# Second mixer of a decoder trunk: which engine splits the weights, which rows are split ahead, and the order of the recurrence's tasks

## The chip, the cores and the metric

One core of a Trainium2 chip runs the whole program. The metric is device time in microseconds (us), the median of several runs; span is the profiled execution from its first to its last instruction.

## The reference

Two layers over 512 positions of width 1024. Each has a mixer and a mixture of experts (MoE). The change is in the mixer of layer 1:

```python
def mixer_rglru(h, w_in, conv_w, conv_b, w_a, b_a, w_x, b_x, lam, w_out):
    gate, xr = jnp.split(h @ w_in, [D_RNN], axis=-1)
    gate = jax.nn.gelu(gate)
    xr = causal_conv(xr, conv_w) + conv_b          # width 4, per channel
    xh = xr.reshape(bsz, t_len, LRU_HEADS, LRU_HEAD_DIM)   # 8 heads of 128
    r = jax.nn.sigmoid(jnp.einsum('bthi,hij->bthj', xh, w_a).reshape(bsz, t_len, D_RNN) + b_a)
    i = jax.nn.sigmoid(jnp.einsum('bthi,hij->bthj', xh, w_x).reshape(bsz, t_len, D_RNN) + b_x)
    log_a = (LRU_C * r.astype(jnp.float32)) * jax.nn.log_sigmoid(lam.astype(jnp.float32))
    a = jnp.exp(log_a)
    b = jnp.sqrt(-jnp.expm1(2.0 * log_a)) * (i * xr).astype(jnp.float32)
    _, hseq = lax.associative_scan(combine, (a, b), axis=1)   # h = a * h + b along positions
    return (gate * hseq.astype(h.dtype)) @ w_out
...
    x = x + mixer_rglru(rms_norm(x, norm_mix_g[1]), ...)      # layer 1
    x = x + hierarchical_moe(rms_norm(x, norm_ffn_g[1]), ...) # 32 experts, 2 of 8 in one of 4 groups
return rms_norm(x, norm_final_g)
```

## The kernel before

Activations lie with channels on the 128 partitions and positions along the row. Dense products keep float32's accuracy by splitting both operands into a high part (rounded to fp32r) and a low part (the rest), and adding three products: high x high, high x low, low x high. The high part of a block of weight rows (`wh`, 128 x 512) is a cast on ScalarE (line 401), the low part (`wl`) a subtraction (line 402) on VectorE or GpSimd, as the argument `lo` says.

The input projection of the second mixer (`mixer1`) has four units of 512 output columns, in the order 2, 3, 0, 1; units 2 and 3 are the recurrence's branch (heads 0 to 3 and 4 to 7), 0 and 1 the gate's. A unit (`unit`) is eight steps, one for each block of 128 weight rows; a step is 12 matmuls (line 445), three products for each of four PSUM banks. Units use banks 0 to 3 and 4 to 7 in turn. Weights come from HBM in halves of a unit (four blocks of rows) through a ring of ten buffers, in the fixed order of a list; an entry for another buffer (`D1`, ...) waits until the program says that it is free.

Tasks of the recurrence are put between the steps: `later` puts a task in a queue with a cost, and after each step `pump` runs tasks until a budget is spent; `flush` runs what is left at the unit's end. `queue` gives the slots by hand, one slot a step. Each engine works its instructions in the order in which they are written, so this sets the order on all engines. For head h the tasks are `c` (bias and taps of the convolution: ScalarE's line 590, three passes of VectorE's line 593 that read the unit's bank), `g` (two gate products in float32, line 601, which reuse banks of the unit before, and two tanh on ScalarE, line 605), `d` (two exponentials on ScalarE, lines 611 and 612, three VectorE passes, 614 to 616), `w` (three VectorE passes, 620 to 622), `roots` (four square roots on ScalarE, line 626, between loads of its function tables) and `s` (a product and the scan on VectorE, 630 and 631). `gated` (`e`) multiplies a scan by its gelu (637 on ScalarE, 638 on VectorE) and splits the result for the output projection (474 on ScalarE, 475).

The output projection (`project`) is made of pieces of 12 matmuls (line 701), by 128 output columns and half of the heads: heads 0 to 3 for columns 0 and 1, then heads 4 to 7 for the same, and so on. The router and the experts of layer 1 follow; their weights (1 MB for each entry) are next in the list, the first for `D1`, which in the mixer holds `xc` of heads 4 to 7. The mixer's buffers have tags: `w0` to `w3` for splits in turn, `q0` to `q3` and `Q` for tanh, `C0`, `C1` and `D0` for the results' high and low parts.

Of the kernel before, what the change touches and what calls it, by code (L numbers as in the profile page):

```python
# [9 lines left out]
F32R = mybir.dt.float32r  # L10
# [3 lines left out]
AF = mybir.ActivationFunctionType  # L14
# [4 lines left out]
P = 128  # L19
T = 512  # L20
NT = 4
D = 1024
NJ = 8
# [16 lines left out]
def hybrid_trunk(ctx: ExitStack, tc: tile.TileContext, x, norm_mix_g, norm_ffn_g, norm_final_g,  # L40
# [5 lines left out]
    V, A, G, TE, SY = nc.vector, nc.scalar, nc.gpsimd, nc.tensor, nc.sync  # L46
# [79 lines left out]
    def take(kind, u):  # L126
        while stream[pos[1]][3] == "C1":
            pos[1] += 1
        k, v, _, _ = stream[pos[1]]
        assert (k, v) == (kind, u), (k, v, kind, u)  # L130
        pos[1] += 1
        t, slot = ring.popleft()
        used.append(slot)
        return t
# [73 lines left out]
    def warm(func):  # L208

        A.activation(dummy, one, func)  # L210
# [125 lines left out]
    class Normed:  # L336
# [23 lines left out]
        def begin(self):  # L360
            wake(3, WAKE[4])
            self.make(0)
            self.make(1)
            for j in range(2, NJ + 1):
                later(lambda j=j: self.make(j), 2)
# [27 lines left out]

    par = [0]

    def split(w, lo):
        par[0] += 1
        shape = [P, *w.shape[1:]]
        wh = big.tile(shape, F32R, tag=f"w{par[0] % 2}", name="wh")
        wl = big.tile(shape, F32R, tag=f"w{par[0] % 2 + 2}", name="wl")  # L400
        A.copy(wh, w)  # L401
        lo.tensor_tensor(wl, w, f(wh), op=OP.subtract)  # L402
        return wh, wl

    first = {}

    def ahead(kind, u, lo=V):

        w = take(kind, u)
        first[kind, u] = w, split(w[:, 0, :], lo)  # L410

    def unit(kind, u, b0, step, budget=1.9, begin=lambda: None, lo=V, then=lambda: None):

        o = [bank(b0 + m, f"pu{m}") for m in range(4)]
        if (kind, u) not in first:
            ahead(kind, u, lo)
        w, nxt = first.pop((kind, u))
        begin()
        for j in range(NJ):
            wh, wl = nxt  # L420
            if j + 1 < NJ:
                if j % 4 == 3:
                    w = take(kind, u)
                nxt = split(w[:, (j + 1) % 4, :], lo)
            else:
                then()
            if j % 4 == 3:
                done()
            step(o, wh, wl, j, j == 0, j == NJ - 1)
            pump(budget)  # L430
        flush()
        return o

    def first_out(kind):
        w = take(kind, 0)
        first[kind, 0] = w, split(w[:, :, 0:P], V)

    def columns_of(n, low=1):

        def step(o, wh, wl, j, first, last):  # L440
            products = [(wh, n.hh), (wl, n.hh)]
            products.insert(low, (wh, n.hl))
            for i, (a, b) in enumerate(products):
                for m in range(4):
                    TE.matmul(o[m], a[:, m * P:(m + 1) * P], b[:, j, :], start=first and i == 0, stop=last and i == 2)  # L445
        return step
# [9 lines left out]
    class Y:  # L456
# [13 lines left out]
        def lo(self, j):  # L470
            return self.part("D0", 4, j) if j < 4 else self.part("JK"[j // 2 - 2], 2, j % 2)
# [98 lines left out]
    def mixer1(rstd):  # L570
        n = Normed(rstd, cols[:, 88:96], 4)
        y = Y()
        step = columns_of(n)
        tags = ("t20", "t21", "sm1", "sm2")
        wax = []

        def recurrence(h0, o):

            hs = range(h0, h0 + 4)
            if h0:  # L580
                d1 = big.tile([P, 4, T], F32, tag="D1", name="xc")
                xc = {h: d1[:, h - h0, :] for h in hs}
            else:
                jk = [big.tile([P, 2, T], F32, tag=t, name="xc") for t in "JK"]
                xc = {h: jk[h // 2][:, h % 2, :] for h in hs}
            tr, ti, tt, ths = {}, {}, {}, []

            def conv(h):
                m = h - h0
                A.activation(xc[h], o[m], AF.Identity, scale=cols[:, 40 + h:41 + h], bias=cols[:, 48 + h:49 + h])  # L590
                for k in (2, 1, 0):
                    d = 3 - k
                    V.scalar_tensor_tensor(xc[h][:, d:], o[m][:, :T - d], cols[:, 16 + 8 * k + h:17 + 8 * k + h],
                                           xc[h][:, d:], op0=OP.mult, op1=OP.add)

            def gates(h):
                if not wax:
                    wax.append(aside.popleft())
                for g, th in enumerate((tr, ti)):
                    pg = bank(h0 + (h - h0) // 2 * 2 + g, "pgate")  # L600
                    TE.matmul(pg, wax[0][:, g, h, :], xc[h], start=True, stop=True)
                    if (h - h0, g) == (2, 0):
                        ths.extend(four(T, "th"))
                    th[h] = ths[2 * (h - h0) + g - 4] if h - h0 > 1 else buf(2 * (h - h0) + g, (T,), "th")
                    A.activation(th[h], pg, AF.Tanh, scale=0.5, bias=half[:, 8 * g + h:8 * g + h + 1])

            def decay(h):


                tt[h] = big.tile([P, T], F32, tag=tags[h - h0], name="tt")  # L610
                A.activation(tt[h], tr[h], AF.Tanh, scale=lc[:, 0, h:h + 1], bias=lc[:, 0, h:h + 1])
                A.activation(tr[h], tr[h], AF.Exp, scale=lc[:, 1, h:h + 1], bias=lc[:, 1, h:h + 1])
                q = tr[h]
                V.tensor_scalar(q, q, 0.5, 0.5, op0=OP.mult, op1=OP.add)
                V.scalar_tensor_tensor(ti[h], ti[h], 1.0, xc[h], op0=OP.add, op1=OP.mult)
                V.scalar_tensor_tensor(xc[h], tt[h], 1.0, q, op0=OP.add, op1=OP.mult)

            def newton(h):
                q = tr[h]
                V.scalar_tensor_tensor(q, xc[h], 2.0, q, op0=OP.subtract, op1=OP.mult)  # L620
                V.tensor_tensor(ti[h], ti[h], q, op=OP.mult)
                V.tensor_scalar(q, q, -2.0, -1.0, op0=OP.mult, op1=OP.add)

            def roots():
                for h in hs:
                    A.activation(tt[h], tt[h], AF.Sqrt)
                warm(AF.Gelu_apprx_tanh if h0 else AF.Exp)

            def scan(h):
                V.scalar_tensor_tensor(ti[h], ti[h], -1.0, tt[h], op0=OP.mult, op1=OP.mult)  # L630
                V.tensor_tensor_scan(xc[h], tr[h], ti[h], 0.0, op0=OP.mult, op1=OP.add)

            return conv, gates, decay, newton, roots, scan, xc

        def gated(h, o, hs, lo=V):
            if h in hs:
                A.activation(o[h % 4], o[h % 4], AF.Gelu_apprx_tanh)
                V.tensor_tensor(hs[h], o[h % 4], hs[h], op=OP.mult)
            if h - 1 in hs:
                y.put(h - 1, hs[h - 1], lo)  # L640

        def queue(*slots):

            for slot in slots:
                for i, t in enumerate(slot):
                    later(lambda t=t: t[0](*t[1:]), 1 if i + 1 == len(slot) else 0)

        o = unit("wi1", 2, 0, columns_of(n, 2), 2.0, n.begin, then=lambda: ahead("wi1", 3, G))
        c, g, d, w, roots, s, hs0 = recurrence(0, o)
        queue([(warm, AF.Exp), (c, 0)], [(c, 1)], [(g, 0), (c, 2)], [(c, 3), (g, 1)], [(d, 0), (w, 0)], [(g, 2), (d, 1), (w, 1)], [(g, 3), (d, 2), (w, 2)], [(d, 3), (w, 3)])  # L650
        o = unit("wi1", 3, 4, step, 1, lo=G, then=lambda: ahead("wi1", 0, G))
        roots0, s0 = roots, s
        c, g, d, w, roots, s, hs1 = recurrence(4, o)
        queue([(c, 4)], [(c, 5)], [(c, 6)], [(roots0,),(c, 7), (s0, 0)], [(g, 4), (s0, 1)], [(g, 5), (s0, 2), (s0, 3)], [(g, 6), (d, 4)], [(g, 7), (d, 5)])
        o = unit("wi1", 0, 0, step, 1, lo=G, then=lambda: ahead("wi1", 1, G))
        e = lambda m, lo=V: (gated, m, o, hs0, lo)
        queue([(d, 6)], [(d, 7), (w, 4)], [(roots,), (w, 5)], [e(0,G), (s, 4)], [e(1,G),(w, 6), (s, 5)], [e(2,G),(w, 7), (s, 6)], [e(3,G),(s, 7)], [e(4,G)])
        o = unit("wi1", 1, 4, step, 1, lo=G, then=lambda: first_out("wo1"))

        def freed():  # L660
            free["D1"] = 1
            prefetch()

        for m in range(4, 9):
            later(lambda m=m, o=o: gated(m, o, hs1), 1.2)
        later(freed, 0)
        return y
# [690 lines left out]
```

## Time and profile before

| what | value |
|---|---|
| median of 3 runs | 1392.84 us (1392.14 to 1394.61) |
| profiled execution | 1395.66 us, span 1394.0 us |
| TensorE busy (PE) | 1325.7 us, 95% of the span |
| VectorE busy (DVE) | 591.2 us, 42% |
| ScalarE busy (ACT) | 347.4 us, 25% |
| GpSimd busy (POOL) | 84.3 us, 6% |
| DMA | 436.95 MB, mean 313 GB/s |

Busy shares are means over stages: the two mixers, the two streams of expert weights, and the stretches between them have different limits. The second mixer's input projection runs from 699 to 812 us of the span.

### The profile page before, as it was taken

What the parts mean: (1) busy time and instruction counts of PE and PEld (TensorE: products, weight loads), DVE (VectorE), ACT (ScalarE), POOL (GpSimd) and SP (SyncE); (2) the same over time, 40 slices, a digit from 0 to 9 for tenths busy, and PEclk for the clock granted to TensorE, in tenths of its full rate; (3) what the DMA queues carried; (4) which work ended last, traced back from release to release, by engine and by line L of the source; (5) the groups of instructions that cost most, each with busy time, mean ns of one, the idle gap of its engine ahead of it and who ended that gap; (6) DMA issues with size and microseconds to landing.
All of it is one profiled execution on the core that took longest, in us unless ns stands there. A gap on an engine that the chain in (4) does not pass through costs nothing. (4 is left out here: it accounts for less than half of the span.)

```text
span 1394.0 us, 16561 instructions
## 1 busy us (share of the span) xinstructions
PE 1325.7 (95%) x6654; PEld 761.1 (55%) x6654; DVE 591.2 (42%) x1104; ACT 347.4 (25%) x581; POOL 84.3 (6%) x65
## 2 busy tenths in 40 slices
PE   8999999999999999998799889899999999999995
PEld 7888874554445544442476568645544455444432
DVE  6455462334423342322468784723333233423225
ACT  4335421221111111110247653212111111111112
POOL 0000100000000000000114332300000000000001
PEclk9999999999999999999899989999999999999998
DMA  9621169899999999999760025598999999999994
GB/s 354 197 101 61 61 232 341 346 409 409 409 408 409 409 409 409 409 409 409 266 228 0 0 78 207 220 344 342 409 409 409 409 409 409 409 409 408 409 409 162
DMA packets 126979, 436.95 MB, mean 313 GB/s; under 512 B 11316, under 2 KB 14000, under 8 KB 126896
## 3 DMA queue, kind: packets, MB, share of 16 engines
q1 hardware_dynamic: 126896, 435.82, 80.4%
q8 instruction: 55, 0.90, 0.3%
q14 instruction: 28, 0.23, 0.0%
HBM read 433.69 MB, written 2.10 MB: 313 GB/s over the span
## 5 line engine op out<-in xcount | busy, mean ns | idle before, releaser
L1018 PE MATMUL pu<-w,xt 128*64 128x512 f32 x1024 | 234.3, 597 | 20.9 <-DMA w<-in_moe_w_up_dram 19.5
L1018 PE MATMUL pg<-w,xt 128*64 128x512 f32 x1024 | 228.8, 597 | 1.2 <-DMA w<-in_moe_w_gate_dram 1.2
L1018 PE MATMUL pd<-w,hT 128*64 128x512 f32 x1024 | 226.8, 595 | 1.4 <-ACT hT L1042 1.4
L1036 DVE SCALAR_TENSOR_TENSOR hid<-pu,gs,sg 128x512 f32<-128x512 f32 x32 | 24.0, 751 | 365.7 <-PE pu L1018 246.9
L1018 PEld LDWEIGHTS pu<-w,xt 128*64 128x64 f32 x1024 | 70.0, 137 | 178.9 <-issue 120.6
L1018 PEld LDWEIGHTS pg<-w,xt 128*64 128x64 f32 x1024 | 72.7, 137 | 145.0 <-issue 134.9
L1018 PEld LDWEIGHTS pd<-w,hT 128*64 128x64 f32 x1024 | 70.7, 137 | 140.4 <-issue 129.4
L880 ACT ACTIVATE xt<-px,gcol 128x256 f32<-128x256 f32 x128 | 60.8, 475 | 303.6 <-PE px L878 303.6
L877 PE MATMUL px<-st,xh 128*128 128x256 f32 x512 | 133.5, 296 | 2.4 <-DVE st L867 2.0
L878 PE MATMUL px<-st,xl 128*128 128x256 f32 x512 | 127.3, 283 | 0.0
L877 PEld LDWEIGHTS px<-st,xh 128*128 128x128 f32 x512 | 98.3, 192 | 30.5 <-issue 26.2
L1058 ACT ACTIVATE y<-pd,gs 128x512 fp32r<-128x512 f32 x64 | 43.8, 687 | 264.7 <-PE pd L1018 263.2
L1059 DVE SCALAR_TENSOR_TENSOR y<-pd,gs,y 128x512 fp32r<-128x512 f32 x64 | 47.9, 751 | 140.4 <-ACT y L1058 138.0
L1003 DVE TENSOR_TENSOR xT<-pc,xT 128x512 f32<-128x512 f32 x128 | 81.5, 686 | 57.4 <-PE pc L1002 57.4
L1003 DVE TENSOR_TENSOR rows<-pc,rows 128x512 f32<-128x512 f32 x128 | 81.4, 685 | 53.5 <-PE pc L1002 53.5
L878 PEld LDWEIGHTS px<-st,xl 128*128 128x128 f32 x512 | 98.4, 192 | 1.6
L401 ACT CAST wh<-w 128x512 fp32r<-128x512 f32 x104 | 64.1, 619 | 69.0 <-PE pu L445 41.4
L402 DVE TENSOR_TENSOR wl<-w,wh 128x512 fp32r<-128x512 f32 x79 | 55.2, 700 | 50.8 <-PE pu L445 26.8
L445 PE MATMUL pu<-hh,wh 128*128 128x512 f32 x256 | 73.7, 409 | 2.7 <-ACT wh L401 2.0
L701 PE MATMUL po<-y,wh 128*128 128x512 f32 (+1 forms) x288 | 70.0, 384 | 5.0 <-ACT y L474 4.0
L1002 PE MATMUL pc<-sp,y 128*128 128x512 f32 x256 | 69.9, 407 | 5.1 <-issue 5.1
L1002 PE MATMUL pc<-y,sp 128*128 128x512 f32 x256 | 68.9, 402 | 2.0 <-DVEq L1154 2.0
(258 smaller groups left out, 1348.5 us busy)
## 6 DMA issues: line engine op xcount, KB each, us to landing
w<-in_moe_w_gate_dram SPq DMA_DIRECT2D x128, 1024.0 KB, 18.3
w<-in_moe_w_up_dram SPq DMA_DIRECT2D x128, 1024.0 KB, 18.4
w<-in_moe_w_down_dram SPq DMA_DIRECT2D x128, 1024.0 KB, 18.3
w<-in_ab_w_in_dram SPq DMA_DIRECT2D x10, 1024.0 KB, 14.9
w<-in_c_w_in_dram SPq DMA_DIRECT2D x8, 1024.0 KB, 10.7
w<-in_ab_w_out_dram SPq DMA_DIRECT2D x4, 1024.0 KB, 10.3
w<-in_c_w_out_dram SPq DMA_DIRECT2D x4, 1024.0 KB
xin<-in_x_dram SPq DMA_DIRECT2D x4, 512.0 KB, 7.2
```

What stands on the lines that cost most here:

```text
L401: A.copy(wh, w)
L402: lo.tensor_tensor(wl, w, f(wh), op=OP.subtract)
L445: TE.matmul(o[m], a[:, m * P:(m + 1) * P], b[:, j, :], start=first and i == 0, stop=last and i == 2)
L701: TE.matmul(o[m, i], w[:, kk, :], part(js[4 * kh + kk])[:, h], start=kh + k + kk == 0, stop=(kh, k, kk) == (1, 2, 3))
L877: TE.matmul(px, self.xh[:, c, j, :], st(c), start=(c == 0), stop=False)
L878: TE.matmul(px, self.xl[:, c, j, :], st(c), start=False, stop=(c == NT - 1))
L880: A.activation(self.xt[q][:, j, :], px, AF.Copy, scale=g)
L1002: TE.matmul(pc, a, b, start=(n == 0), stop=(n == 1))
L1003: V.tensor_tensor(d, pc, d, op=OP.add)
L1018: TE.matmul(o[64 * s:64 * s + 64, :], xt[:, 64 * s:64 * s + 64], w[s][:, j, wide], start=first, stop=last)
L1058: A.activation(yh[s], pd[s], AF.Copy, scale=by(0))
L1059: V.scalar_tensor_tensor(yl[s], pd[s], by(0), f(yh[s]), op0=OP.mult, op1=OP.subtract)
```

## The change

`split` can write into buffers that it is given, `ahead` can split any row block of a unit, and `unit` uses what is there. In the second mixer:

- Low parts of weights are made on VectorE, apart from six that the code gives to GpSimd (`G`): rows 3 and 4 of unit 3, rows 2 to 5 of unit 0. Low parts of results (line 475) go to VectorE too.
- Blocks of rows are split ahead into buffers that lie idle: rows 0 to 2 of unit 3 and rows 0 and 1 of unit 0 at the end of unit 2 (into `D1`, `C0`, `D0`), the other early rows as tasks between steps.
- Tasks move: the square roots of heads 0 to 3 go to the end of unit 3, the scans of those heads stand between the taps of heads 4 to 7, taps come ahead of gates within a slot, and most `d`, `w` and `s` are a step earlier. The load of ScalarE's Exp table moves to the start of unit 2.

The number of products, splits and tasks is the same.

```diff
@@ -393,37 +393,42 @@
 
     par = [0]
 
-    def split(w, lo):
-        par[0] += 1
-        shape = [P, *w.shape[1:]]
-        wh = big.tile(shape, F32R, tag=f"w{par[0] % 2}", name="wh")
-        wl = big.tile(shape, F32R, tag=f"w{par[0] % 2 + 2}", name="wl")
+    def split(w, lo, into=None):
+        if into:
+            wh, wl = into
+        else:
+            par[0] += 1
+            shape = [P, *w.shape[1:]]
+            wh = big.tile(shape, F32R, tag=f"w{par[0] % 2}", name="wh")
+            wl = big.tile(shape, F32R, tag=f"w{par[0] % 2 + 2}", name="wl")
         A.copy(wh, w)
         lo.tensor_tensor(wl, w, f(wh), op=OP.subtract)
         return wh, wl
 
-    first = {}
-
-    def ahead(kind, u, lo=V):
-
-        w = take(kind, u)
-        first[kind, u] = w, split(w[:, 0, :], lo)
-
-    def unit(kind, u, b0, step, budget=1.9, begin=lambda: None, lo=V, then=lambda: None):
+    first, halves, rows_ahead = {}, {}, {}
+
+    def row_of(kind, u, j):
+
+        if (kind, u, j // 4) not in halves:
+            halves[kind, u, j // 4] = take(kind, u)
+        return halves[kind, u, j // 4][:, j % 4, :]
+
+    def ahead(kind, u, lo=V, j=0, into=None):
+
+        rows_ahead[kind, u, j] = split(row_of(kind, u, j), lo, into)
+
+    def unit(kind, u, b0, step, budget=1.9, begin=lambda: None, lo=lambda j: V, then=lambda: None):
 
         o = [bank(b0 + m, f"pu{m}") for m in range(4)]
-        if (kind, u) not in first:
-            ahead(kind, u, lo)
-        w, nxt = first.pop((kind, u))
+        if (kind, u, 0) not in rows_ahead:
+            ahead(kind, u, lo(0))
         begin()
         for j in range(NJ):
-            wh, wl = nxt
-            if j + 1 < NJ:
-                if j % 4 == 3:
-                    w = take(kind, u)
-                nxt = split(w[:, (j + 1) % 4, :], lo)
-            else:
+            wh, wl = rows_ahead.pop((kind, u, j))
+            if j + 1 == NJ:
                 then()
+            elif (kind, u, j + 1) not in rows_ahead:
+                ahead(kind, u, lo(j + 1), j + 1)
             if j % 4 == 3:
                 done()
             step(o, wh, wl, j, j == 0, j == NJ - 1)
@@ -645,17 +650,48 @@
                 for i, t in enumerate(slot):
                     later(lambda t=t: t[0](*t[1:]), 1 if i + 1 == len(slot) else 0)
 
-        o = unit("wi1", 2, 0, columns_of(n, 2), 2.0, n.begin, then=lambda: ahead("wi1", 3, G))
+        def begin():
+            warm(AF.Exp)
+            n.begin()
+
+        shelves = {}
+
+        def put_ahead(u, j, lo=V):
+
+            if j == 0:
+                shelves[u] = [big.tile([P, 4, T], F32R, tag=t, name="ahead") for t in ("C0", "D0")]
+            hi, lw = shelves[u]
+            ahead("wi1", u, lo, j, (hi[:, j], lw[:, j]))
+
+        def while_idle():
+
+            both = big.tile([P, 4, T], F32R, tag="D1", name="ahead")
+            ahead("wi1", 3)
+            for j in (1, 2):
+                ahead("wi1", 3, V, j, (both[:, j - 1], both[:, j + 1]))
+            row_of("wi1", 3, 4)
+            put_ahead(0, 0)
+            put_ahead(0, 1)
+
+        def early(u, j):
+            ahead("wi1", u, G, j)
+
+        o = unit("wi1", 2, 0, columns_of(n, 2), 2.0, begin, then=while_idle)
         c, g, d, w, roots, s, hs0 = recurrence(0, o)
-        queue([(warm, AF.Exp), (c, 0)], [(c, 1)], [(g, 0), (c, 2)], [(c, 3), (g, 1)], [(d, 0), (w, 0)], [(g, 2), (d, 1), (w, 1)], [(g, 3), (d, 2), (w, 2)], [(d, 3), (w, 3)])
-        o = unit("wi1", 3, 4, step, 1, lo=G, then=lambda: ahead("wi1", 0, G))
-        roots0, s0 = roots, s
+        p = put_ahead
+        queue([(c, 0), (early, 3, 3)], [(c, 1), (early, 3, 4)], [(c, 2), (g, 0), (p, 0, 2, G)],
+              [(c, 3), (p, 0, 3, G), (g, 1), (d, 0), (w, 0)], [(g, 2), (d, 1), (w, 1)], [(g, 3), (d, 2), (w, 2)],
+              [(d, 3), (w, 3)], [(roots,)])
+        o = unit("wi1", 3, 4, step, 1)
+        s0 = s
         c, g, d, w, roots, s, hs1 = recurrence(4, o)
-        queue([(c, 4)], [(c, 5)], [(c, 6)], [(roots0,),(c, 7), (s0, 0)], [(g, 4), (s0, 1)], [(g, 5), (s0, 2), (s0, 3)], [(g, 6), (d, 4)], [(g, 7), (d, 5)])
-        o = unit("wi1", 0, 0, step, 1, lo=G, then=lambda: ahead("wi1", 1, G))
-        e = lambda m, lo=V: (gated, m, o, hs0, lo)
-        queue([(d, 6)], [(d, 7), (w, 4)], [(roots,), (w, 5)], [e(0,G), (s, 4)], [e(1,G),(w, 6), (s, 5)], [e(2,G),(w, 7), (s, 6)], [e(3,G),(s, 7)], [e(4,G)])
-        o = unit("wi1", 1, 4, step, 1, lo=G, then=lambda: first_out("wo1"))
+        queue([(c, 4), (s0, 0)], [(c, 5), (s0, 1), (early, 0, 4)], [(c, 6), (g, 4), (early, 0, 5)],
+              [(c, 7), (g, 5), (s0, 2), (s0, 3)], [(g, 6), (d, 4), (p, 1, 0)], [(g, 7), (d, 5), (p, 1, 1)],
+              [(d, 6), (w, 4), (p, 1, 2)], [(d, 7), (w, 5), (p, 1, 3)])
+        o = unit("wi1", 0, 0, step, 1)
+        e = lambda m: (gated, m, o, hs0)
+        queue([(roots,), (w, 6)], [(w, 7), (s, 4)], [(s, 5), e(0)], [(s, 6), e(1)], [(s, 7), e(2)], [e(3)], [e(4)])
+        o = unit("wi1", 1, 4, step, 1, then=lambda: first_out("wo1"))
 
         def freed():
             free["D1"] = 1
```

What this makes of VectorE's queue is seen at three places (an instruction's line, its kind, what it writes and reads; names with numbers are PSUM banks of a unit). The first is unit 3, where taps are done and decay and newton of heads 0 and 1 follow. Before:

```order
L593 SCALAR_TENSOR_TENSOR xc<-pu_4921,cols,xc 128x509
L614 TENSOR_SCALAR th<-th 128x512
L615 SCALAR_TENSOR_TENSOR th<-th,xc 128x512
L616 SCALAR_TENSOR_TENSOR xc<-tt,th 128x512
L620 SCALAR_TENSOR_TENSOR th<-xc,th 128x512
L621 TENSOR_TENSOR th<-th 128x512
L622 TENSOR_SCALAR th<-th 128x512
L614 TENSOR_SCALAR th<-th 128x512
L615 SCALAR_TENSOR_TENSOR th<-th,xc 128x512
L616 SCALAR_TENSOR_TENSOR xc<-tt,th 128x512
```

And after the change:

```order
L598 SCALAR_TENSOR_TENSOR xc<-pu_4921,cols,xc 128x509
L619 TENSOR_SCALAR th<-th 128x512
L620 SCALAR_TENSOR_TENSOR th<-th,xc 128x512
L621 SCALAR_TENSOR_TENSOR xc<-tt,th 128x512
L625 SCALAR_TENSOR_TENSOR th<-xc,th 128x512
L626 TENSOR_TENSOR th<-th 128x512
L627 TENSOR_SCALAR th<-th 128x512
L405 TENSOR_TENSOR wl<-w,wh 128x512
L619 TENSOR_SCALAR th<-th 128x512
L620 SCALAR_TENSOR_TENSOR th<-th,xc 128x512
L621 SCALAR_TENSOR_TENSOR xc<-tt,th 128x512
```

A low part of weights now stands behind each head's decay and newton, and the first pass of the next head stands behind it.

The second is unit 0, taps of heads 4 to 7 and scans of heads 0 to 3. Before, from the second tap of head 6 on:

```order
L593 SCALAR_TENSOR_TENSOR xc<-pu_5098,cols,xc 128x510
L593 SCALAR_TENSOR_TENSOR xc<-pu_5098,cols,xc 128x509
L593 SCALAR_TENSOR_TENSOR xc<-pu_5099,cols,xc 128x511
L593 SCALAR_TENSOR_TENSOR xc<-pu_5099,cols,xc 128x510
L593 SCALAR_TENSOR_TENSOR xc<-pu_5099,cols,xc 128x509
L630 SCALAR_TENSOR_TENSOR th<-th,tt 128x512
L631 SCALAR_TENSOR_TENSOR xc<-th 128x512
L630 SCALAR_TENSOR_TENSOR th<-th,tt 128x512
L631 SCALAR_TENSOR_TENSOR xc<-th 128x512
```

And after, from the first tap of head 4 on:

```order
L598 SCALAR_TENSOR_TENSOR xc<-pu_5108,cols,xc 128x511
L598 SCALAR_TENSOR_TENSOR xc<-pu_5108,cols,xc 128x510
L598 SCALAR_TENSOR_TENSOR xc<-pu_5108,cols,xc 128x509
L635 SCALAR_TENSOR_TENSOR th<-th,tt 128x512
L636 SCALAR_TENSOR_TENSOR xc<-th 128x512
L598 SCALAR_TENSOR_TENSOR xc<-pu_5109,cols,xc 128x511
L598 SCALAR_TENSOR_TENSOR xc<-pu_5109,cols,xc 128x510
L598 SCALAR_TENSOR_TENSOR xc<-pu_5109,cols,xc 128x509
L635 SCALAR_TENSOR_TENSOR th<-th,tt 128x512
L636 SCALAR_TENSOR_TENSOR xc<-th 128x512
L598 SCALAR_TENSOR_TENSOR xc<-pu_5110,cols,xc 128x511
L598 SCALAR_TENSOR_TENSOR xc<-pu_5110,cols,xc 128x510
```

The scans of heads 0 and 1 have moved ahead of the taps of heads 5 and 6.

The third is unit 1, from the first gated product on. Before:

```order
L638 TENSOR_TENSOR xc<-pu_5311,xc 128x512
L630 SCALAR_TENSOR_TENSOR th<-th,tt 128x512
L631 SCALAR_TENSOR_TENSOR xc<-th 128x512
L638 TENSOR_TENSOR xc<-pu_5312,xc 128x512
L620 SCALAR_TENSOR_TENSOR th<-xc,th 128x512
L621 TENSOR_TENSOR th<-th 128x512
L622 TENSOR_SCALAR th<-th 128x512
L630 SCALAR_TENSOR_TENSOR th<-th,tt 128x512
L631 SCALAR_TENSOR_TENSOR xc<-th 128x512
L638 TENSOR_TENSOR xc<-pu_5313,xc 128x512
```

And after, from the scan of head 4 on:

```order
L635 SCALAR_TENSOR_TENSOR th<-th,tt 128x512
L636 SCALAR_TENSOR_TENSOR xc<-th 128x512
L635 SCALAR_TENSOR_TENSOR th<-th,tt 128x512
L636 SCALAR_TENSOR_TENSOR xc<-th 128x512
L643 TENSOR_TENSOR xc<-pu_5319,xc 128x512
L405 TENSOR_TENSOR wl<-w,wh 128x512
L635 SCALAR_TENSOR_TENSOR th<-th,tt 128x512
L636 SCALAR_TENSOR_TENSOR xc<-th 128x512
L643 TENSOR_TENSOR xc<-pu_5320,xc 128x512
L480 TENSOR_TENSOR y<-xc,y 128x512
L405 TENSOR_TENSOR wl<-w,wh 128x512
```

Newtons have left this stretch, and low parts of weights (405) and of results (480) have come in, each behind a scan and a gated product.

## Rows read from the trace of the kernel before

**Rows 1.** Windows: us; PE, PEld, DVE, ACT, POOL busy (instructions); granted clock, DMA share, GB/s.
```profile
750.00:786.00 36.00, 31.41 (x114) 21.52 (x113) 30.25 (x35) 19.74 (x31) 13.53 (x9) 0.95 0.00 0
786.00:812.50 26.50, 24.23 (x97) 18.80 (x95) 24.13 (x27) 17.20 (x29) 14.16 (x10) 0.94 0.00 1
812.50:826.70 14.20, 9.53 (x27) 6.62 (x28) 13.56 (x19) 9.26 (x15) 3.94 (x2) 0.76 0.00 1
...
1000.00:1350.00 350.00, 341.40 (x1728) 162.02 (x1726) 116.28 (x201) 53.19 (x93) 0.00 (x0) 1.00 1.03 409
```

**Rows 2.** Timeline of TensorE: start, duration, engine, line, what, count.
```profile
721.02 1.07 PE L445 MATMUL pu<-hh,wh 128*128 128x512 f32 x4
...
723.74 1.07 PE L445 MATMUL pu<-hh,wh 128*128 128x512 f32 x4
...
729.19 1.88 PE L601 MATMUL pgate<-xc,w 128*128 128x512 f32 x4
...
731.84 1.08 PE L445 MATMUL pu<-hl,wh 128*128 128x512 f32 x4
...
811.22 1.07 PE L445 MATMUL pu<-hh,wl 128*128 128x512 f32 x4
...
826.67 2.18 PE L701 MATMUL po<-y,wh 128*128 128x512 f32 x8
```

**Rows 3.** Timeline: two waits and the blocks behind one (in brackets: idle before, releaser).
```profile
772.79 1.27 ACT L605 ACTIVATE th<-pgate,half 128x512 f32<-128x512 f32 x2 [8.21 <-DVE xc L631]
...
799.50 1.19 PE L445 MATMUL pu<-hh,wh 128*128 128x512 f32 x4 [1.98 <-ACT wh L401]
...
804.87 1.07 PE L445 MATMUL pu<-hl,wh 128*128 128x512 f32 x4
```

**Rows 4.** Timeline: one instruction of VectorE beside a split on GpSimd, and alone.
```profile
738.95 1.62 POOL L402 TENSOR_TENSOR wl<-w,wh 128x512 fp32r<-128x512 f32 x1 [0.77 <-ACT wh L401]
...
739.53 1.58 DVE L616 SCALAR_TENSOR_TENSOR xc<-tt,th 128x512 f32<-128x512 f32 x1
...
758.36 0.69 DVE L616 SCALAR_TENSOR_TENSOR xc<-tt,th 128x512 f32<-128x512 f32 x1
```

**Rows 5.** Groups of VectorE's instructions by shape, 735 to 812 us: busy, mean ns.
```profile
L616 DVE SCALAR_TENSOR_TENSOR xc<-tt,th 128x512 f32<-128x512 f32 x8 | 10.9, 1367 | 0.8
L631 DVE TENSOR_TENSOR_SCAN xc<-th 128x512 f32<-128x512 f32 x6 | 9.3, 1543 | 0.2
L620 DVE SCALAR_TENSOR_TENSOR th<-xc,th 128x512 f32<-128x512 f32 x7 | 7.2, 1033 | 0.1
```

**Rows 6.** Page and timeline: durations of the tasks' instructions.
```profile
L402 DVE TENSOR_TENSOR wl<-w,wh 128x512 fp32r<-128x512 f32 x79 | 55.2, 700 | 50.8 <-PE pu L445 26.8
...
731.11 0.69 ACT L605 ACTIVATE th<-pgate,half 128x512 f32<-128x512 f32 x1 [0.17 <-PE pgate L601]
...
736.69 0.82 ACT L611 ACTIVATE tt<-th,lc 128x512 f32<-128x512 f32 x1
...
761.85 8.98 DVE L593 SCALAR_TENSOR_TENSOR xc<-pu,cols,xc 128x511 f32<-128x511 f32 x12
761.90 1.28 ACT L210 ACT_TABLE_LOAD   x1
...
770.75 0.68 DVE L630 SCALAR_TENSOR_TENSOR th<-th,tt 128x512 f32<-128x512 f32 x1
...
772.61 0.67 DVE L630 SCALAR_TENSOR_TENSOR th<-th,tt 128x512 f32<-128x512 f32 x1
...
794.96 0.42 DVE L614 TENSOR_SCALAR th<-th 128x512 f32<-128x512 f32 x1
...
798.48 0.69 DVE L620 SCALAR_TENSOR_TENSOR th<-xc,th 128x512 f32<-128x512 f32 x1
```

**Rows 7.** Timeline of ScalarE: gelu of heads 4 and 5, cast of the last result.
```profile
821.63 1.07 ACT L637 ACTIVATE pu<-pu 128x512 f32<-128x512 f32 x2
...
826.75 0.62 ACT L474 CAST y<-xc 128x512 fp32r<-128x512 f32 x1 [0.60 <-DVE xc L638]
```

## The prediction

> **What bounds the kernel now.** I read the table by stage first [rows 1]. Behind the second mixer the kernel streams expert weights at 409 GB/s with TensorE all but full [rows 1]; nothing there is touched, and the first expert product waits for the router, the router for the output projection, and that for the mixer. The queue of expert weights opens when the last gated product has read D1, so it moves with the mixer. Whatever the mixer ends earlier, the program ends earlier, one for one. The question is when the third piece of the output projection (the first that reads heads 4 to 7) starts: 826.67 now [rows 2].
>
> Next, how much of that is TensorE's own work. A step of twelve products takes 723.74 - 721.02 = 2.72 us. A pair of gate products takes 1.74: it starts at 729.19, and the block behind it at 731.84 - 0.91 = 730.93 [rows 2]. Units 3, 0 and 1 from 721.02 are 24 steps and 8 gate pairs, 65.3 + 13.9 = 79.2 us: an end at 800.2. The last block starts at 811.22 and ends at 812.13: 11.9 us are waiting. Two pieces of the projection at 2.72 and 0.3 for the router's bias would bring the third piece at 805.9; it comes at 826.67. So at most 20.8 us can be had.
>
> Then, who makes TensorE wait. In its table VectorE is busy 84% of the stretch of unit 0, 91% of unit 1's and 95% of the projection's start, and the granted clock falls to 0.95, 0.94 and 0.76 of the upper level of 2.4 GHz, so part of the time runs at the lower, 1.2 GHz [rows 1]. The chain of the waits agrees: at 772.79 ScalarE's tanh of head 4 had idled 8.21 us for a scan of the first heads on VectorE, since it writes into that head's buffer, and TensorE idles behind it [rows 3]. At 799.50 TensorE had waited 1.98 us for a high part that stands in ScalarE's queue behind a square root which needs VectorE [rows 3]. The bound is VectorE's queue, and ScalarE's where it depends on it.
>
> Last, why VectorE is slow. The same instruction, L616, takes 1.58 us beside a split on GpSimd (738.95 to 740.57) and 0.69 at 758.36, alone [rows 4]. From 735 to 812 us the eight L616 average 1.367, the seven L620 1.033, the six scans 1.543 [rows 5], against 0.69, 0.69 and 1.23 alone: 5.4 + 2.4 + 1.9 = 9.7 us in three lines.
>
> **The change, by parts.** Prices, start to start [rows 6]: a low part on VectorE 0.70; taps of four heads 8.98, so 2.25 each; scan with its product 772.61 - 770.75 = 1.86; decay and newton together 798.48 - 794.96 = 3.52, about half each; the second tanh starts 1.92 after the gate pair (731.11 - 729.19) and takes 0.69; the two exponentials 0.82 each; a table load 1.28. ScalarE's cast I take as 0.6, a square root as 0.7, as its other passes of that size.
>
> Low parts: of 24 weight splits and 4 results that GpSimd takes in the middle of this mixer, 6 splits stay there. VectorE gets 22 passes of 0.70, 15.4 us, and is rid of the contention. The six remaining run beside taps, which read one operand from PSUM; at 0.75 each over a row in which GpSimd works too [rows 6], taps pay nothing. Bound: 0 to 0.9 each; I take 0.
>
> Five splits at the end of unit 2 (one already there): 3.5 us on VectorE and 2.4 on ScalarE ahead of the first taps. They are hidden: all are done by 722.7, the Exp table is now loaded ahead of unit 2, and the first gate product does not come before 729.19.
>
> Unit 3: ahead rows cover steps 1 to 4; rows 5 to 7 are split on VectorE, each behind one decay and newton, which wait for tanh and exponentials. Second gate pair at 721.02 + 4 x 2.72 + 1.74 = 733.64; exponential done 733.64 + 1.92 + 0.69 + 1.64 = 737.9; decay and newton to 741.4, low part of row 5 at 742.1. Step 5 starts at 739.8 and wants it 1.81 later, at 741.6: 0.5 late. The same sum for row 6 gives 746.6, just in time. For row 7: fourth gate pair 743.0, exponential 747.25, decay and newton 750.8, low part 751.5, wanted at 749.7: 1.8 late. Unit 3 ends at 752.45 instead of 721.02 + 8 x 2.72 + 4 x 1.74 = 749.7. Here the change costs 2.7 us.
>
> Unit 0: head 3's decay is done at 751.5 + 1.75 = 753.3; square root, table load, Identity of head 4: 756.2; taps 758.5, scan of head 0 760.3, taps of head 5 762.6, scan 764.4, heads 6 and 7 768.9, two scans 772.7. TensorE, three steps from 752.45, wants the second gate product of head 4 at 761.5 and gets its bank at 762.6: 1.1 late, in place of the old wait for the scan, which is now ahead. The third pair starts at 770.7, but its tanh takes the four-buffer tile of heads 2 and 3, free at 772.7; queued behind it are the exponentials of head 4, done 775.6. Decay 777.35, two splits 778.75. The exponentials of head 5 end at 779.6, decay and two splits 782.75. Step 7 starts 0.9 late for its cast and 0.5 more for this split: unit 0 ends at 783.7.
>
> Unit 1: rows 0 to 3 are ahead. VectorE has no gap from 782.75 on: two decays and four newtons 10.6, fifteen passes of 0.70 (splits, gated products, low parts of results) 10.5, four scans 7.4, together 28.5: the low part for the projection's first piece at 811.25. In this order row 4's low part comes at 799.85, wanted at 783.7 + 4 x 2.72 + 1.81 = 796.4: 3.4 late. Rows 5 and 6 come at 803.8 and 807.75, 1.3 and 1.2 late; row 7 in time. Unit 1 ends at 811.4, only 0.7 earlier than now, but the results of heads 0 to 3 are then done. ScalarE's way on is the old one: result 3 at 809.1, a cast, a table load, a cast that needs step 7's buffer (812.0), a table load, gelu of head 4 at 813.3, against 821.63 now. From there the results take the same 5.1 us to the last cast (826.75) [rows 7], so the third piece comes 8.3 us earlier.
>
> **The clock.** A wait can cost twice. Behind the 1.98 us wait four blocks took 804.87 - 799.50 = 5.37 us instead of 3.63 [rows 3]: 1.74 lost. The new 1.8 us wait in unit 3 may cost the same; 1.1 of it would disappear in the wait for head 5's bank, and through the tanh some 0.4 comes through. Behind the 3.4 us wait VectorE is late for the next two steps anyway, which covers it. Sum: 8.3 - 0.4 = 7.9 us, so a span of 1386.1. The profiled execution took 1395.66 for a span of 1394.0; the median of the runs is 1392.84, 2.8 less. Taken off that: **1384.9 us**.
>
> The Trainium skill, "TensorE: Matmul & The Clock Gate", section "HAM oscillation — how this bites in real kernels", says that waits which recur between groups of matmuls send the array back to its low clock each time, and that the loss is paid at every such wait. By that rule the four longer waits above (1.8, 3.4, 1.3, 1.2) would each cost the 1.74 and the sum would be 8.3 - 7.0 = 1.3; by the rows it is 7.9, since a later wait hides the loss. It is the second rival.
>
> **The rivals.** *VectorE is never late.* If its passes run closer than start to start in the old trace, or the scheduler's waits are looser than I read them, TensorE comes near its floor: 13 to 20.8 us, about 1375. For it: it idles some 3 us ahead of head 4's decay in my sum. Against: the 28.5 us without a gap in unit 1. Chance 0.10.
>
> *The clock takes it back.* Four waits at 1.74, not hidden: 1391.5. For it: at 799.50 the loss was seen. Against: VectorE's late passes lie over it. It decides from three unhidden losses on. Chance 0.14.
>
> *The slow passes are slow by themselves.* If the 9.7 us of excess in [rows 5] has nothing to do with GpSimd, it stays, all of it in VectorE's queue after 735, on top of the passes taken over: 9.7 - 7.9 = 1.8 us slower, and over 4 with the shorter lines that I left out, 1395 to 1397. It decides once 80% of the excess stays. Against: 1.58 and 0.69 for one instruction [rows 4]. Chance 0.06.
>
> *Nothing arrives.* An earlier mixer meets weights that aren't there. Against: D1 comes free with the last result, and the rest of the path to the first expert is unchanged. Chance 0.04, same time.
>
> **The numbers.** The forecast, a gain of 4 to 13 us, has 0.66. Faster and slower mean by over 0.2%, 2.8 us, about what a measurement of this kernel can tell from no change. Faster: 0.66 + 0.10 + a third of the clock's 0.14, 0.80; same 0.13; slower 0.07. The low end, 1377, lets a gain of 16 in; the high end, 1391, most of the clock's case.
>
> **What the profile will show.** L616, L620 and the scans at their times alone; TensorE waiting for a low part from VectorE at unit 3's last step (1.8 us) and unit 1's fifth (3.4 us); no wait of 8 us ahead of head 4's tanh; the third piece near 818.4. If the waits at those two steps are missing, the gain is larger; if VectorE's means stay, or the clock is below 0.9 through unit 1 and the third piece comes after 823, I am wrong on the other side.

## The result, and the profile after

| kernel | median of its runs | profiled execution | span |
|---|---|---|---|
| before | 1393.07 us (4 runs) | 1395.66 us | 1394.0 us |
| changed | 1384.92 us (4 runs) | 1385.47 us | 1383.8 us |

The ratio of the changed kernel to the one before is 0.9934, 95% interval 0.992 to 0.9947: about 9 us faster. The forecast was 1384.9 us. One execution each of two experiments below took far longer than the others, 1599.45 and 3992.96 us; they are left out of the medians and ratios.

The changed kernel's profiled execution comes to the second mixer 2.1 us sooner than the other (first product at 696.99 against 699.10), ahead of anything that was changed. So places in the mixer are compared by their distance from that first product. The forecast went by the third piece of the output projection. It starts at 814.58, 117.6 us behind the first product instead of 127.6, but waits once inside, so the fourth piece is taken here: it starts at 818.02, 121.03 us behind the first product; before it was 829.62, 130.52 behind. The mixer is 9.5 us shorter. TensorE, before:

```profile
699.10 1.16 PE L445 MATMUL pu<-hh,wh 128*128 128x512 f32 x4 [0.26 <-DVE hh L354]
...
813.67 0.97 PE L701 MATMUL po<-y,wh 128*128 128x512 f32 x3 [0.76 <-ACT wh L401]
818.35 2.08 PE L701 MATMUL po<-y,wh 128*128 128x512 f32 x4 [3.71 <-ACT y L474]
...
829.62 2.03 PE L701 MATMUL po<-y,wh 128*128 128x512 f32 x8
```

Most of the gain lies in the projection's first three pieces, which hardly wait for results any more: from its first product to the fourth piece they took 829.62 - 813.67 = 15.95 us and now take 818.02 - 808.88 = 9.14. What lies ahead of it is 2.7 us shorter.

The table by stage, for units 3, 0 and 1 and the projection's first two pieces (columns as in [rows 1]):

```profile
721.00:752.50 31.50, 29.32 (x111) 20.30 (x110) 22.77 (x37) 19.87 (x31) 4.53 (x4) 1.00 0.00 1
752.50:784.00 31.50, 30.14 (x116) 21.10 (x115) 25.85 (x37) 20.34 (x31) 2.58 (x2) 1.00 0.00 1
784.00:812.00 28.00, 25.56 (x104) 20.10 (x103) 25.52 (x40) 16.30 (x28) 0.00 (x0) 0.94 0.00 1
812.00:819.00 7.00, 6.61 (x29) 5.03 (x28) 5.55 (x9) 5.69 (x10) 0.00 (x0) 1.00 0.19 39
```

GpSimd has gone from 13.53 us in 36 and 14.16 in 26.5 [rows 1] to 2.58 and nothing, and VectorE, with more passes, is still busy 82% and 91% of its two main stretches. The stretch of unit 0 took 36 us and now takes 31.5. The projection's start, 14.2 us at a clock of 0.76 before, is now at full clock in the stretch from 812 on.

VectorE's groups by shape, 735 to 812 us, answer to [rows 5]:

```profile
L636 DVE TENSOR_TENSOR_SCAN xc<-th 128x512 f32<-128x512 f32 x8 | 9.8, 1224 | 0.3
L621 DVE SCALAR_TENSOR_TENSOR xc<-tt,th 128x512 f32<-128x512 f32 x8 | 5.5, 692 | 0.7
L625 DVE SCALAR_TENSOR_TENSOR th<-xc,th 128x512 f32<-128x512 f32 x8 | 5.5, 688 | 0.1
```

The three lines that averaged 1.543, 1.367 and 1.033 us (scan, decay's last pass, newton's first) are at 1.224, 0.692 and 0.688: their times alone.

TensorE's timeline, at the places where it waits or passes from unit to unit:

```profile
696.99 1.17 PE L450 MATMUL pu<-hh,wh 128*128 128x512 f32 x4 [0.26 <-DVE hh L354]
...
740.31 1.20 PE L450 MATMUL pu<-hh,wl 128*128 128x512 f32 x4 [0.36 <-DVE wl L405]
...
749.93 1.20 PE L450 MATMUL pu<-hh,wl 128*128 128x512 f32 x4 [1.75 <-DVE wl L405]
750.97 1.10 PE L450 MATMUL pu<-hh,ahead 128*128 128x512 f32 x4
751.90 1.09 PE L450 MATMUL pu<-hl,ahead 128*128 128x512 f32 x4
...
761.15 1.10 PE L606 MATMUL pgate<-xc,w 128*128 128x512 f32 x2 [0.77 <-ACT th L610]
...
782.09 1.10 PE L450 MATMUL pu<-hh,ahead 128*128 128x512 f32 x4
...
797.69 1.31 PE L450 MATMUL pu<-hh,wl 128*128 128x512 f32 x4 [2.44 <-DVE wl L405]
798.80 1.91 PE L450 MATMUL pu<-hh,wh 128*128 128x512 f32 x4
800.51 1.79 PE L450 MATMUL pu<-hl,wh 128*128 128x512 f32 x4
802.13 1.09 PE L450 MATMUL pu<-hh,wl 128*128 128x512 f32 x4
...
804.98 1.20 PE L450 MATMUL pu<-hh,wl 128*128 128x512 f32 x4
...
808.88 2.12 PE L737 MATMUL po<-y,wh 128*128 128x512 f32 x8
...
814.58 0.86 PE L737 MATMUL po<-y,wh 128*128 128x512 f32 x3
815.83 1.44 PE L737 MATMUL po<-y,wh 128*128 128x512 f32 x5 [0.39 <-ACT y L479]
...
818.02 2.02 PE L737 MATMUL po<-y,wh 128*128 128x512 f32 x8
```

Unit 0 starts at 750.97 and unit 1 at 782.09. The waits stand where low parts come late from VectorE: the last step of unit 3, the fifth of unit 1. Before, TensorE waited 3.23 us ahead of head 5's gates (773.53), behind the 8.21 us of [rows 3]; that is gone, and 0.77 us at head 4's second gate is left.

What VectorE itself still waits for, and its queue in unit 1 (waits, 735 to 780 us: total, times, longest; then timeline):

```profile
DVE th L619 <- ACT th L617: 7.4, 4, 2.9
...
773.94 0.43 DVE L619 TENSOR_SCALAR th<-th 128x512 f32<-128x512 f32 x1 [2.94 <-ACT th L617]
...
780.92 0.42 DVE L619 TENSOR_SCALAR th<-th 128x512 f32<-128x512 f32 x1
...
782.58 0.69 DVE L625 SCALAR_TENSOR_TENSOR th<-xc,th 128x512 f32<-128x512 f32 x1
783.30 0.69 DVE L626 TENSOR_TENSOR th<-th 128x512 f32<-128x512 f32 x1
...
803.64 0.68 DVE L480 TENSOR_TENSOR y<-xc,y 128x512 fp32r<-128x512 f32 x1
804.24 0.68 DVE L405 TENSOR_TENSOR wl<-w,wh 128x512 fp32r<-128x512 f32 x1
...
807.25 0.68 DVE L405 TENSOR_TENSOR wl<-w,wh 128x512 fp32r<-128x512 f32 x1
```

Line 617 is a decay's exponential on ScalarE; the other ScalarE pass of a decay, line 616 (611 before), is a tanh, though the parts ahead of the result call both exponentials. Four times the first pass of a decay on VectorE waits for line 617, 7.4 us in all. From 780.92 to the projection's first low part at 807.25 there is no gap.

### The profile page after: what moved, and what is told of

Read it like the earlier page. It is cut to its first block, busy times and chain, and to the rows that moved or that the text cites. A ratio compares the mean times of both kernels' runs of the same rounds, so it can differ in the third digit from the quotient of the medians.

```text
span 1383.8 us, 16540 instructions
## 1 busy us (share of the span) xinstructions
PE 1319.3 (95%) x6654; PEld 756.5 (55%) x6654; DVE 586.9 (42%) x1126; ACT 347.2 (25%) x581; POOL 49.4 (4%) x43
## 5 line engine op out<-in xcount | busy, mean ns | idle before, releaser
L405 DVE TENSOR_TENSOR wl<-w,wh 128x512 fp32r<-128x512 f32 x89 | 60.9, 687 | 51.9 <-PE pu L450 26.8
L404 ACT CAST wh<-w 128x512 fp32r<-128x512 f32 x94 | 58.0, 620 | 63.9 <-PE pu L450 37.7
L1070 ACT ACTIVATE sg<-pg,gs 128x512 f32<-128x512 f32 x32 | 22.0, 688 | 193.3 <-PE pg L1054 186.2
```

## The experiments

The theory: VectorE's queue sets the mixer's length. The change shortens it by taking away the contention with GpSimd, and uses it better through order and early splits. Rivals: one part alone is the gain; or TensorE's own waits in the changed kernel are paid for. The kernel before was timed again beside the first four experiments and beside the last four, with medians of 1393.88 and 1394.08 us; the changed kernel was not, so experiments are set against it by ratio and by the mixer's length. That length is from one execution of each kernel.

| kernel | median, us | ratio to before (95%) | first product, fourth piece | mixer, us |
|---|---|---|---|---|
| before | 1393.07 | 1 | 699.10, 829.62 | 130.5 |
| VectorE only | 1390.21 | 0.9973 (0.9962 to 0.9984) | 700.71, 825.76 | 125.1 |
| order only | 1390.1 | 0.9974 (0.9964 to 0.9985) | 697.41, 824.07 | 126.7 |
| order and VectorE, no rows ahead | 1387.12 | 0.995 (0.9937 to 0.9963) | 697.97, 820.64 | 122.7 |
| order and rows ahead, GpSimd | 1389.53 | 0.9965 (0.9952 to 0.9978) | 697.40, 822.76 | 125.4 |
| changed | 1384.92 | 0.9934 (0.992 to 0.9947) | 696.99, 818.02 | 121.0 |
| changed, decay ahead of gates | 1379.77 | 0.9897 (0.988 to 0.9913) | 698.40, 814.20 | 115.8 |
| changed, six more on VectorE | 1386.12 | 0.9944 (0.9929 to 0.9959) | 697.77, 819.45 | 121.7 |
| changed, row 4 of unit 1 early | 1386.33 | 0.995 (0.9933 to 0.9968) | 698.14, 819.20 | 121.1 |
| both of these moves | 1379.95 | 0.9899 (0.9882 to 0.9916) | 699.07, 814.90 | 115.8 |

**Order and rows ahead, low parts on GpSimd.** The changed kernel with the engine put back:

```diff
-        o = unit("wi1", 3, 4, step, 1)
+        o = unit("wi1", 3, 4, step, 1, lo=lambda j: G)
...
-        e = lambda m: (gated, m, o, hs0)
+        e = lambda m: (gated, m, o, hs0, G)
```

(the same for units 0 and 1 and the rows ahead)

> The changed order and the rows split ahead stay; all low parts of weights of units 3, 0 and 1 and the low parts of the results of heads 0 to 3 go back to GpSimd. My theory (VectorE's queue bounds the mixer, and a split on GpSimd costs VectorE about as much as it saves, since passes with two SBUF operands stretch beside it): VectorE loses 22 passes of 0.6 to 0.7 us (13 to 15 us) and gets 10 to 16 us of stretching back, and GpSimd's low parts take 1.3 to 1.7 us instead of 0.7; so 1386 to 1391 us, 1 to 6 slower than the changed kernel. Rival (stretching doesn't matter, only VectorE's number of passes): 1373 to 1379 us, since the 22 passes leave the bounding queue.

1389.53 us, inside the theory's interval. A group by shape, TensorE's longest waits in units 0 and 1, and VectorE from head 6's decay to the gated product of head 3:

```profile
L621 DVE SCALAR_TENSOR_TENSOR xc<-tt,th 128x512 f32<-128x512 f32 x8 | 10.9, 1362 | 0.8
...
761.29 1.11 PE L606 MATMUL pgate<-xc,w 128*128 128x512 f32 x2 [3.04 <-DVE xc L598]
...
802.88 1.82 PE L450 MATMUL pu<-hh,wh 128*128 128x512 f32 x4 [4.10 <-ACT wh L404]
...
782.40 1.50 DVE L619 TENSOR_SCALAR th<-th 128x512 f32<-128x512 f32 x1
...
807.21 1.26 DVE L643 TENSOR_TENSOR xc<-pu,xc 128x512 f32<-128x512 f32 x2
```

The decay's last pass is back at 1.362 us, as before; scans and newton's first pass come back in part (1.344 and 0.824 us). VectorE takes 808.47 - 782.40 = 26.1 us from head 6's decay to the end of head 3's gated product. In the changed kernel it takes 24.6 (780.92 to 805.53), with seven low parts more in between. So the number of its passes alone is not what counts. About 1.1 us of the loss are there before: head 6's decay begins 782.40 - 697.40 = 85.0 us behind the first product instead of 83.9, after TensorE has waited 3.04 us in unit 0 with two blocks at the lower level of the clock behind that (granted clock 0.56 from 761.83 to 765.62).

**VectorE only.** The kernel before with `lo=G` and `e(.., G)` taken out of `mixer1`:

```diff
-        o = unit("wi1", 3, 4, step, 1, lo=G, then=lambda: ahead("wi1", 0, G))
+        o = unit("wi1", 3, 4, step, 1, then=lambda: ahead("wi1", 0))
```

(the same for the other units and for `e`)

> The kernel before with one thing changed: low parts of weights and results in the second mixer are all made on VectorE; order of tasks as before, no rows ahead. Theory: VectorE's busy time stays about the same (stretching gone, passes added), but the low parts now stand behind taps, decays and scans in its queue and the wait of head 4's tanh for the first heads' scans stays: 1391 to 1397 us, no gain over before. Rival (the engine that makes the low parts is the whole gain): 1383 to 1387 us.

1390.21: faster than expected. A group by shape, TensorE's longest waits, and the tanh of head 4 on ScalarE:

```profile
L616 DVE SCALAR_TENSOR_TENSOR xc<-tt,th 128x512 f32<-128x512 f32 x8 | 5.5, 692 | 0.4
...
755.54 1.19 PE L445 MATMUL pu<-hh,wl 128*128 128x512 f32 x4 [1.55 <-DVE wl L402]
...
759.79 1.20 PE L445 MATMUL pu<-hh,wl 128*128 128x512 f32 x4 [1.23 <-DVE wl L402]
...
773.44 1.27 ACT L605 ACTIVATE th<-pgate,half 128x512 f32<-128x512 f32 x2 [3.79 <-DVE xc L631]
...
813.21 2.08 PE L445 MATMUL pu<-hh,wl 128*128 128x512 f32 x4 [2.37 <-DVE wl L402]
```

L616 falls to 0.692 with nothing else changed, so the stretching comes from GpSimd. My error was the wait of head 4's tanh: with VectorE quicker through the first heads it is 3.79 us instead of 8.21 and no longer holds TensorE up, even in the old order. TensorE now waits for low parts, as expected: up to 1.55 us in units 3 and 0, and 2.37 us for the last one of unit 1.

**Order and VectorE, no rows ahead.** The changed kernel without `early`, `p` and `while_idle`:

```diff
-        queue([(c, 4), (s0, 0)], [(c, 5), (s0, 1), (early, 0, 4)], [(c, 6), (g, 4), (early, 0, 5)],
+        queue([(c, 4), (s0, 0)], [(c, 5), (s0, 1)], [(c, 6), (g, 4)],
```

> The changed kernel without any row split ahead: each row is split one step ahead as before, all low parts on VectorE, tasks in the changed order. Theory: the first steps of units 3 and 0 now carry a low part each beside taps and scans (in unit 0 2.25 + 1.86 + 0.7 = 4.8 us of VectorE for a step of 2.72), so TensorE waits some 2 us in each of three steps there and again in unit 1: 1387 to 1395 us, 2 to 10 slower than the changed kernel. Rival (splitting ahead adds nothing, VectorE has the same passes anyway): 1384 to 1386 us.

1387.12, at the theory's lower end: of the waits of some 2 us in three steps of unit 0, TensorE had one, of 1.23 us (754.98). By the mixer's length the rows ahead are worth 122.7 - 121.0 = 1.7 us; the intervals of the two ratios overlap.

**Order only.** As the last, with low parts on GpSimd:

```diff
-        o = unit("wi1", 0, 0, step, 1)
+        o = unit("wi1", 0, 0, step, 1, lo=lambda j: G, then=lambda: ahead("wi1", 1, G))
```

(the same for the other units and for `e`)

> Only the order of the tasks from the change (square roots, scans among the taps, taps ahead of gates, Exp table early): low parts on GpSimd as before, no rows ahead. Theory: the wait of head 4's tanh for the first heads' scans goes, with the 5 us that it and the low clock behind it cost TensorE, but VectorE stays stretched: 1386 to 1391 us. Rival (order is the whole gain): 1383 to 1386 us; rival (order is nothing without the engine): 1392 to 1394.

1390.1, as the theory had it. Head 4's wait is gone, but others have come: high parts that stand in ScalarE's queue behind the square roots.

```profile
755.32 1.97 PE L450 MATMUL pu<-hh,wh 128*128 128x512 f32 x4 [3.87 <-ACT wh L404]
...
792.98 2.08 PE L450 MATMUL pu<-hh,wh 128*128 128x512 f32 x4 [3.77 <-ACT wh L404]
```

So in ratio the engine alone gives 0.27%, the order alone 0.26%, both 0.50%, rows ahead the rest of 0.66%. No part is the whole gain. In ratio, order and engine add up; by the mixer's length they overlap a little (5.4 and 3.8 us alone, 7.8 together). The rows ahead bring 0.09% with GpSimd and 0.16% with VectorE, which the intervals don't separate from nothing or from each other.

**Decay ahead of the next gates.** One move more, to take VectorE's 7.4 us of waiting away: for five of the eight heads, the decay's two ScalarE passes go ahead of the gate products and tanh of a later head.

```diff
-              [(c, 3), (p, 0, 3, G), (g, 1), (d, 0), (w, 0)], [(g, 2), (d, 1), (w, 1)], [(g, 3), (d, 2), (w, 2)],
+              [(c, 3), (p, 0, 3, G), (d, 0), (g, 1), (w, 0)], [(d, 1), (g, 2), (w, 1)], [(d, 2), (g, 3), (w, 2)],
...
-              [(c, 7), (g, 5), (s0, 2), (s0, 3)], [(g, 6), (d, 4), (p, 1, 0)], [(g, 7), (d, 5), (p, 1, 1)],
+              [(c, 7), (g, 5), (s0, 2), (s0, 3)], [(d, 4), (g, 6), (p, 1, 0)], [(d, 5), (g, 7), (p, 1, 1)],
```

> The changed kernel with one more move: in each slot the decay of a head (two exponentials on ScalarE) is queued ahead of the next head's gate products and tanh; VectorE's own order stays the same. Theory: VectorE's queue sets the mixer, and in the changed kernel it idles 7.4 us ahead of line 619 for exponentials that stand in ScalarE's queue behind the next head's tanh. Without that the row 7 low part of unit 3 comes in time (its 1.75 us wait goes), and everything from head 4 on comes 4 to 6 us earlier: 1378 to 1381 us, 4 to 6 faster than the changed kernel. Rival (TensorE's product stream, not VectorE's queue, sets the mixer now): the 1.75 us of unit 3 at most, 1383 to 1385 us.

1379.77 us, ratio 0.9897 (0.988 to 0.9913), 5.2 us below the changed kernel in the mixer and about as much in the median. TensorE's last low part of unit 3, then ScalarE, VectorE and the wait in question:

```profile
748.38 1.08 PE L450 MATMUL pu<-hh,wl 128*128 128x512 f32 x4
...
766.21 0.82 ACT L617 ACTIVATE th<-th,lc 128x512 f32<-128x512 f32 x1
769.09 1.26 ACT L610 ACTIVATE th<-pgate,half 128x512 f32<-128x512 f32 x2 [2.06 <-DVE xc L636]
...
768.91 0.40 DVE L619 TENSOR_SCALAR th<-th 128x512 f32<-128x512 f32 x1
...
DVE th L619 <- ACT th L617: 1.6, 2, 0.8
...
793.87 1.19 PE L450 MATMUL pu<-hh,wl 128*128 128x512 f32 x4 [1.63 <-DVE wl L405]
```

Head 4's exponential is done at 767.03, ahead of the tanh that waits for a buffer, and VectorE goes from scan to decay without a gap. Its waits ahead of line 619 fall from 7.4 to 1.6 us, and the mixer gets 5.2 of those 5.8. TensorE's 1.75 us wait at unit 3's last low part is gone, as expected. Instructions, their engines, and the orders on VectorE and TensorE are those of the changed kernel; the rival of TensorE's products had 1.75 us at most. This version beats both kernels.

**The last six on VectorE too.**

```diff
-            ahead("wi1", u, G, j)
+            ahead("wi1", u, V, j)
```

(and `p` for rows 2 and 3 of unit 0)

> The changed kernel with the six low parts that GpSimd kept (rows 3 and 4 of unit 3, 2 to 5 of unit 0) on VectorE too. The prediction put the six at no cost beside taps and VectorE idle at those places. Theory: within 1 us of the changed kernel if that idle time takes them, up to 2.5 slower where two of them stand among taps and scans in unit 0: 1384.5 to 1387. Rival (GpSimd stretches the taps and the six are a cost): 1381 to 1383 us.

1386.12, in the theory's interval; the mixer is 0.7 us longer. The six on GpSimd cost nothing that shows, and taken over they cost nearly nothing.

**Row 4 of unit 1 early.** TensorE's longest new wait taken away where it stood:

```diff
-              [(d, 6), (w, 4), (p, 1, 2)], [(d, 7), (w, 5), (p, 1, 3)])
+              [(d, 6), (w, 4), (p, 1, 2)], [(d, 7), (w, 5), (p, 1, 3), (ahead, "wi1", 1, V, 4)])
```

> The changed kernel with the low part of row 4 of unit 1 made ahead of the newtons of heads 6 and 7, so TensorE's longest new wait (2.4 us idle at unit 1's fifth step, and the low clock behind it) is taken away there. Theory: VectorE's passes up to the last low part of unit 1 are the same in number and have no gap, so the wait moves to the next step and the time stays within 0.7 us of the changed kernel: 1384 to 1385.5. Rival (the wait and its low clock are paid): 2.4 to 4 us faster, 1380.5 to 1382.5 us.

1386.33, with an interval that includes the changed kernel's ratio; the mixer is 121.1 us long, as against 121.0. The time lies 0.8 us above the theory's 1384 to 1385.5, on the side away from the rival. The wait has moved a step on:

```profile
796.31 1.07 PE L450 MATMUL pu<-hh,wl 128*128 128x512 f32 x4
800.10 2.07 PE L450 MATMUL pu<-hh,wh 128*128 128x512 f32 x4 [2.72 <-ACT wh L404]
```

It is now for the high part of row 5, behind a result's cast that needs VectorE's gated product. In a stretch in which VectorE has no gap, moving the wait did not remove it.

**Both moves.** The two edits above together.

> Both of the moves before: decay ahead of the next gates, and row 4's low part of unit 1 early. Theory: as the first alone within 0.7 us, 1378 to 1381 us. Rival (the wait in unit 1 is paid): 2 to 4 us below the first.

1379.95 us and a mixer of 115.8 us: the same as the first alone, in line with the theory. TensorE's longest wait in unit 1:

```profile
795.80 1.20 PE L450 MATMUL pu<-hh,wh 128*128 128x512 f32 x4 [1.96 <-ACT wh L404]
```

## Why the prediction came out

**What bounds.** VectorE's queue, with ScalarE's where it depends on it. Shown: taking its idle time away (decay ahead of gates) brought 5.2 us; taking its passes away but bringing GpSimd back lost 4.4 in the mixer (125.4 against 121.0), 1.1 of them ahead of VectorE's full stretch.

**Contention.** Shown in both directions: 0.692 us with all low parts on VectorE in the old order, 1.362 with GpSimd in the new. The rival that these passes are slow by themselves falls. The trace of before shows more than the prediction read in it:

```profile
745.64 1.60 POOL L402 TENSOR_TENSOR wl<-w,wh 128x512 fp32r<-128x512 f32 x1 [5.07 <-ACT wh L401]
746.22 1.57 DVE L616 SCALAR_TENSOR_TENSOR xc<-tt,th 128x512 f32<-128x512 f32 x1
...
758.73 1.48 POOL L402 TENSOR_TENSOR wl<-w,wh 128x512 fp32r<-128x512 f32 x1 [1.36 <-ACT wh L401]
```

All six long L616 began while a split ran on GpSimd, and each ended 0.54 or 0.55 us behind that split's end (here 747.79 and 747.24; in [rows 4] 741.11 and 740.57), as if it had been held until then and not slowed. The one at 758.36 was not alone, as I wrote: a split began 0.37 us behind its start, and it was not held. In these rows, then, what counts is which of the two begins first.

**Unit 3.** Waits of 0.5 and 1.8 us were forecast, 0.36 and 1.75 came. By distance from the first product the unit was to end at 752.45 - 699.10 = 53.35 us, and it ended at 750.97 - 696.99 = 53.98. The change costs time in this unit, as forecast.

**Unit 0.** 783.7 - 752.45 = 31.25 forecast, 782.09 - 750.97 = 31.12 measured. VectorE's idle time ahead of head 4's decay, 775.6 - 772.7 = 2.9 in the sum, is 2.94. The wait at head 4's second gate was 0.77, not 1.1; the profile names the tanh, which ended at 761.11, but head 5's taps ended at 761.00, so the bank that I named was as late within 0.1.

**Unit 1.** Mis-sized: the 28.5 us of VectorE without a gap are 807.85 - 780.92 = 26.9 (the low part at 807.25 with its 0.60). Passes that don't depend on each other follow at 0.60 (803.64 to 804.24), not at 0.70, and fifteen of them make 1.5 us. The rival in which VectorE is never late had this right, but the waits did not go away. Row 4's low part was 2.44 us late instead of 3.4, and gelu of head 4 came 9.5 us earlier by distance (810.04 - 696.99 = 113.05 against 122.53), not 8.3.

**The clock.** The term of 0.4 us was wrong: behind the 1.75 us wait the blocks follow at 0.93 (750.97 to 751.90), and the granted clock of that stretch is 1.00. Behind the 2.44 us wait two blocks took 802.13 - 798.80 = 3.33 instead of 1.82, at the lower level (granted clock 0.53 from 798.80 to 802.20), and a clock of 0.94 stands in the table. That this loss lies under VectorE's lateness was argued, and the rows bear it out: at 804.98 TensorE takes row 6's low part, which VectorE had made at 804.24 + 0.68 = 804.92, so there VectorE is the later again. Rows 5 and 6, forecast 1.3 and 1.2 us late, brought next to no wait of their own. The rival in which the clock takes the gain back falls. It was drawn from the Trainium skill, "TensorE: Matmul & The Clock Gate", section "HAM oscillation — how this bites in real kernels", with the loss paid at every wait. The waits that the section describes are of about 3 to 5 us, longer than most of those to which I applied it; the trace agrees for the 2.44 us wait and not for the 1.75 us one, and the measurement decides.

**The sum.** 7.9 us forecast, 9.5 in the mixer and 8 to 9 in the runs (1393.07 - 1384.92 = 8.2; the ratio gives 9.2). The two errors, 1.5 and 0.4 us too little gain, would make 9.8; unit 3, which ended 0.6 us later than forecast, takes some of it back. So that the median met the forecast to 0.02 us is luck. The span fell by 10.2 us for 2.1 + 9.5 = 11.6 at the fourth piece. The first expert product starts 12.6 us sooner (880.16 against 892.80), so the rival of weights that have not arrived falls too. By the end 2.4 us of that are gone again; how stays open, and runs of one kernel differ by as much.

## What to carry to other kernels

When an engine's queue sets a stretch, ask two things of each of its passes: what stretches it (here a split running on GpSimd held it until it was done), and what it waits for in another engine's queue. An instruction that unblocks the bounding engine belongs ahead of one that may itself wait: a decay's tanh and exponential, put ahead of a later head's tanh at five places, were worth 5 us with no other edit, over half of what the whole change brought. A wait of TensorE inside a stretch where another engine has no gap was a symptom here: moving it changed nothing.

## What the hardware showed that I had not expected

Two passes of VectorE of 0.68 us each, 128 x 512, follow one another at 0.60 us when the second doesn't need the first's result (803.64, 804.24), while those of a dependent chain follow at 0.72 (782.58, 783.30). A sum by recorded durations is 0.08 us too long for each independent pass. TensorE's wait of 1.75 us left the granted clock at 1.00, while one of 2.44 us was followed by two blocks at the lower level. Waits of nearly one length came out differently: with both moves a wait of 1.96 us left the clock at 1.00 (795.70 to 799.50), and before, one of 1.98 us was followed by 0.57 (800.50 to 803.60).
